# RWKV's y in a hybrid decoder step: products with the state over 128 rows, a decay vector per head, and other scheduling numbers

## The chip, the core and the metric

One core of one Trainium2 chip runs the whole program. The metric is the time of one execution in microseconds. The median of three runs before the change is 1459.84 us (1459.55 to 1460.57). Names of engines: PE is the matmul engine (PEld its weight loads), DVE the vector engine, ACT the activation engine, POOL the general-purpose engine, SP the engine that issues all DMAs here.

## What is computed

One layer of a decoder with two branches on the same input: gated linear attention (GLA) and RWKV-7. Their outputs are gated, projected up, merged, projected out and normalised. The prompt has 1024 tokens of 1024 columns; 8 sample tokens ride along. The branch that the change touches is the recurrence of RWKV-7, with 16 heads of 64:

```python
def _rwkv7_scan(r, w, k, v, kk, a, S0):
    def step(S, inp):
        rt, wt, kt, vt, kkt, at = inp
        sa = jnp.einsum('bhvk,bhk->bhv', S, -kkt)
        S = S * wt[:, :, None, :] + sa[..., None] * (kkt * at)[:, :, None, :] + vt[..., None] * kt[:, :, None, :]
        y = jnp.einsum('bhvk,bhk->bhv', S, rt)
        return S, y
    ...
p = jnp.einsum('btd,dn->btn', x, w_in)
...
y, S_rwkv = _rwkv7_scan(rh, hr(w), kh, vh, kk, hr(a), S_rwkv0.astype(jnp.float32))
```

`p` is the projection of x by w_in (9360 columns); by far the most matmuls of the kernel are this projection.

## The kernel before

**Passes and blocks.** The tokens are taken in two passes of 512 (PASS; the first has the 8 sample tokens as well). In each pass w_in is worked off in blocks of 128 columns (`blocks`). A block is 24 matmuls per stretch of tokens: each fp32 operand is split into two fp32r parts (xh and xl, and w's two parts in wpart), and three products are made for each of 8 row tiles. The first pass takes stretches of 256 and 264 tokens, the second one of 512. After both passes come the up-projections and the output projection.

**The pairs.** The 16 heads are handled as 8 pairs per pass, so 16 pairs in all. A pair's 128 partitions are two heads of 64 (HS). Time is cut into chunks of C = 64 tokens, NCH = 8 of them per pass. A pair runs through four parts:
- `front` (L1167 on): decays and keys on DVE and ACT; AZ, BK and `pc`, the decay over a whole chunk, [128, 8] (L1215); the products BK by AZ on PE (big<-az,wide in the profile); then the inversion of a triangular matrix per chunk. For that the 32x32 blocks go through HBM (LD by SP's DMAs into a tile of tag wide), POOL runs 62 instructions (tiles X and Xt), and the result goes back through HBM (XD) into XT and Yd.
- `back`: DVE transposes blocks of XT into Xd, PE multiplies (big<-Xd,Ld, then big<-Yd,Xt), and DVE multiplies AZ by `pc` into GG (tag gg).
- `turn`: transposes.
- `chain` (L1342 on): the recurrence over the 8 chunks. Each step has three matmuls of 128x130 in the one bank pch, with an evacuation between them: pch<-wide,gg gives `rh` (ACT or DVE copies it), pch<-rh,XT gives `u` (two copies of 64x65, one per head), and pch<-wide gives the state's change. Beside them ACT computes the decayed state s0 = u * pc (gg<-wide,pc in the profile), which DVE adds to the third product. After the 8 steps y is made by 32 matmuls in one bank: for each chunk and head one with the state (L1377, big<-az,gg) and one with u (L1379, big<-gg,wide).

The product with the state takes, for head h, only the 64 rows of that head: `d.s0[hs, x, ...]` by `AZ[hs, x, 1]`, a form of the PE array of 64 rows by 64 columns. The product with u takes all 128 rows by 64 columns, since GG holds zeros where it must.

**What sets the order.** The five engines run instruction streams that are fixed when the program is built. `Order.run` builds them: generators (streams) offer one operation each, and the one with the lowest key is issued next. The key is the modelled start time, less a priority (PRIO, FOR_PE), with additions for changes of the PE array's form (SWITCH), table loads of ACT (TABLE, AGE) and other things (ASIDE, URGENT, BIAS). `E` operations may go to DVE or POOL, `C` operations to ACT or DVE: the one that would end earlier by the model takes them. Nearly every instruction is issued by one helper and has the line L227 in the profile, so groups are told apart by their tiles.

Of the kernel before, what the change touches and what calls it, by code (L numbers as in the profile page):

```python
# [14 lines left out]
AF = mybir.ActivationFunctionType  # L15
# [5 lines left out]
P = 128  # L21
# [5 lines left out]
HT = TP // 2  # L27
# [5 lines left out]
C = 64  # L33
CV = C + 1
NCH = HT // C
# [10 lines left out]
HALF = HT + NS  # L46
SBUF = {
    "row": ([P, HALF], 40), "wide": ([P, NCH * 2 * CV], 4), "gg": ([P, NCH * 4 * CV], 2), "lw": ([P, HT], 2),
    "l2s": ([P, 2 * P], 1), "pc": ([P, NCH], 3), "az": ([P, 2 * HT], 2), "X": ([P, 256], 1),
    "Xt": ([P, P], 1), "Ld": ([P, P], 2), "S": ([P, GDV], 2), "Sp": ([P, CV], 2), "rh": ([P, 2 * CV], 2), "vm": ([P, NCH], 2),  # L50
    "sto": ([P, P], 1), "bnd": ([P, 1], 3), "st": ([P, 32], 3), "part": ([P, HALF], 2), "l2p": ([P, 2 * P], 2),
    "pair": ([P, 2, HT // 32], 3),
# [13 lines left out]
IDLE = 3  # L66
RANKW, RANKM = 48, 66
SPARE_ROWS = 11
EARLY_GATES = 13


HOP = {"P": 0.2, "D": 0.418, "G": 0.115, "V": 0.064, "A": 0.14}
# [2 lines left out]
HOLD = 0.11  # L75
TABLE = 1.28

AGE = 1.045

SPARE = 0.411  # L80
LANDED = 0.648
BIAS = 0.193
ASIDE = 8.388

PRIO = {"evacuate": 0.39, "pair": 0.3, "turn": 0.5, "chain": 0.42, "norm": 0.1, "x": 0.61, "lora": 0.42, "rank":
        1.25, "head": 0.27, "gate": -0.38, "w": 0.3, "out": 0.04, "state": -0.13, "block": -0.38}
FOR_PE = {"pair": 1.0, "turn": 1.84, "chain": 0.8, "norm": 0.39, "lora": 0.29, "rank": 1.85, "head": 0.89, "gate":
        1.0, "state": 2.11, "out": 0.05}
STAND, SCARCE, PER_ROW = 0.034, 0.249, 0.148

URGENT = 1.707
SIGMOID, EXP = "sigmoid_and_others", "natural_log_exp_and_others"
SETS = {AF.Sigmoid: SIGMOID, AF.Tanh: SIGMOID, AF.Exp: EXP, AF.Ln: EXP}

HS = (slice(0, 64), slice(64, 128))
# [144 lines left out]
def together(ops):  # L240

    op = ops[0]
    fns = [x.fn for x in ops]
    op.ways = [(op.eng, lambda: [fn() for fn in fns], sum(x.cost for x in ops))]
    op.ins = [y for x in ops for y in x.ins]
    op.outs = [x.out for x in ops]
    op.eng, op.fn, op.cost = op.ways[0]
    return op


class Stream:
# [4 lines left out]
    def be(self, name):  # L256
        self.kind, self.prio, self.for_pe = name, PRIO[name], FOR_PE.get(name, 0.0)


class Order:  # L260
# [83 lines left out]
    def start(self, op):  # L344

        best = None
        for eng, fn, cost in op.ways:
# [17 lines left out]
            if len(op.ways) > 1:  # L365
                end += BIAS if eng == "V" and "A" in op.ways[0][0] else ASIDE if eng == "G" and "G" in op.port else 0.0
            if best is None or end < best[0]:
# [13 lines left out]
    def run(self):  # L381
        while self.streams:
# [3 lines left out]
            for s in before:  # L386
                self.advance(s)
                if s.op is not None:
# [5 lines left out]
                    if s.kind in self.urgent:  # L394
                        key -= URGENT
                    if s.op.table not in (None, self.table):
                        key += max(0.0, TABLE - AGE * s.op.late)
                    if best is None or key < best[0]:
# [32 lines left out]
class Kern(Order):  # L431
# [735 lines left out]
    def front(self, c, p, st, d):  # L1167
        a, A, V, E = self.a, self.A, self.V, self.E
        BK_, L_ = yield from self.get("wide", 2)
        az, gg = (yield from self.get("az")), (yield from self.get("gg"))  # L1170
        BK = BK_[:, :2 * HT].rearrange("p (c t) -> p c t", c=NCH)
        AZ, g4 = az.rearrange("p (c s t) -> p c s t", c=NCH, s=2), gg.rearrange("p (c k z) -> p c k z", c=NCH, k=2)
# [12 lines left out]
        def bc(ap):  # L1185
            return ap.rearrange("p (c t) -> p c t", t=C)
        ta, tb, td, te, Pc_ = yield from self.rows(5)
        ts, tb, Pc_ = (x[:, :NCH * (C + 1)] for x in (ta, tb, Pc_))
        ta, td, te = (x[:, :HT] for x in (ta, td, te))
        ts3, tb3, Pc = (x.rearrange("p (c t) -> p c t", t=C + 1) for x in (ts, tb, Pc_))  # L1190
# [21 lines left out]
        yield V.scalar_tensor_tensor(td, td, -1.0, ta, ALU.mult, ALU.mult)  # L1212
        yield E.tensor_mul(kb, kb, te)
        yield E.tensor_mul(AZ[:, :, 1], bc(r), Pc[:, :, 1:])
        pc = yield from self.get("pc")  # L1215
        yield E.tensor_copy(pc, tb3[:, :, 0])

        for h, hs in enumerate(HS):
            yield E.tensor_mul(BK[hs, :, h * C:h * C + C], bc(td)[hs], tb3[hs, :, 1:])
# [16 lines left out]
        for n, y in enumerate(p4):  # L1236
            x, h = H * (n // 2), n % 2
# [9 lines left out]
        Ld_ = yield from self.get("Ld")  # L1247
# [7 lines left out]
        X = X_.rearrange("p (i t) -> p i t", t=32)  # L1255
# [13 lines left out]
        XT = (yield from self.get("XT")).rearrange("p (c h t) -> p c h t", c=NCH, h=2)  # L1269
# [5 lines left out]
        Yd_ = yield from self.get("Yd")  # L1275
        Yd = Yd_.rearrange("p (g x t) -> p g x t", g=4, t=32)
        H = NCH // 2
        for q in range(2):
# [3 lines left out]
                yield self.S.dma_start(XT[HS[h]][b, :, h, b], XD[n * NCH:(n + 1) * NCH].rearrange("c s t -> s c t"))  # L1282
            for x in range(0 if q else H):
                yield self.S.dma_start(Yd[32 * x:32 * x + 32, :, x], XD[2 * NCH + x:4 * NCH:H].rearrange("g s t -> s g t"))
        d.AZ, d.BK, d.G, d.XT, d.v, d.bonus, d.pc, d.L, d.Ld, d.Yd = AZ, BK, GG, XT, st[2], st[1], pc, L_, Ld_, Yd_
        d.y = Pc_[:, :HT]

    def back(self, d):
        GG, XT = d.G, d.XT

        H = NCH // 2
        Xd_ = yield from self.get("Xd")
        Xd = Xd_.rearrange("p (x g t) -> p x g t", g=4, t=32)
        q = [slice(32 * n, 32 * n + 32) for n in range(4)]
        for h in range(2):
            for n in range(2):
                g = 2 * h + n
                yield self.V.transpose(Xd[q[g], :, g], XT[q[2 * h], H * n:H * n + H, h, 0:32])
        pA = yield from self.bank("big", [P, P])
        yield together([self.P.matmul(pA[q[x]], d.Ld[:, x * 32:x * 32 + 32], Xd_[:, x * P:x * P + P], start=True, stop=True)  # L1300
                        for x in range(H)])
        As = yield from self.get("Xt")
        yield self.C.copy(As, pA)
        self.free(pA, Xd_, d.Ld)
        pZ = yield from self.bank("big", [P, P])
        yield together([self.P.matmul(pZ[q[g]], As[:, g * 32:g * 32 + 32], d.Yd[:, g * P:g * P + P], start=True, stop=True)
                        for g in range(4)])
        pZ3 = pZ.rearrange("p (x t) -> p x t", t=32)
        for h in range(2):
            for n in range(2):  # L1310
                yield self.C.copy(XT[q[2 * h], H * n:H * n + H, h, 32:64], pZ3[q[2 * h + n]])

        for h, hs in enumerate(HS):
            yield self.E.tensor_mul(GG[hs, :, 0, h], d.AZ[hs, :, 0], d.pc[hs].unsqueeze(2).to_broadcast([C, NCH, C]))
        self.free(pZ, As, d.Yd)

    def turn(self, d):
# [24 lines left out]
    def chain(self, c, p, d):  # L1342
        A, V = self.A, self.V
        AZ, BK, GG, XT, pc = d.AZ, d.BK, d.G, d.XT, d.pc
        u_, bt_ = d.u, BK

        for h, hs in enumerate(HS):
            if c.i:
                yield self.S.dma_start(u_[hs, 0, h], self.Sp[p][hs])
            else:  # L1350
                yield self.E.memset(u_[hs, 0, h], 0.0)
        S = yield from self.get("Sp")
        uf = u_.rearrange("p c h v -> p c (h v)")

        for x in range(NCH):
            u, s0 = u_[:, x], d.s0[:, x].rearrange("p (h v) -> p h v", h=2)
            pr = yield from self.bank("pch", [P, 2, CV])
            yield self.P.matmul(pr, GG[:, x, 0], u, start=True, stop=True)
            rh = yield from self.get("rh")
            yield self.C.copy(rh, pr.rearrange("p h v -> p (h v)"))  # L1360
            self.free(pr)
            yield A.activation(s0, u, AF.Copy, scale=pc[:, x:x + 1])
            pu = yield from self.bank("pch", [P, 2, CV])
            yield self.P.matmul(pu, XT[:, x], rh, start=True, stop=True)
            self.free(rh)
            for h, hs in enumerate(HS):
                yield self.C.copy(u[hs, h], pu[hs, h])
            self.free(pu)
            pS = yield from self.bank("pch", [P, 2, CV])
            yield self.P.matmul(pS, bt_[:, x], u, start=True, stop=True)  # L1370
            for h, hs in enumerate(HS):
                un = u_[hs, x + 1, h] if x + 1 < NCH else S[hs]
                yield V.tensor_add(un, pS[hs, h], s0[hs, h])
            self.free(pS)
        pY = yield from self.bank("big", [P, NCH, C])
        vs = [slice(1 + h * C, 1 + h * C + C) for h in range(2)]
        yield together([self.P.matmul(pY[hs, x], d.s0[hs, x, vs[h]], AZ[hs, x, 1], start=(x == 0), stop=False, skip_group_check=True)  # L1377
                        for x in range(NCH) for h, hs in enumerate(HS)] +
                       [self.P.matmul(pY[hs, x], uf[:, x, vs[h]], GG[:, x, 1, h], start=False, stop=True, skip_group_check=True)  # L1379
                        for x in range(NCH) for h, hs in enumerate(HS)])  # L1380
        yield self.C.copy(d.y, pY.rearrange("p c t -> p (c t)"))
        self.free(pY)
        self.free(AZ, BK, u_, GG, XT, pc)
        if c.i:
            self.spawn(self.state(p, S), "state")
        else:
            yield self.S.dma_start(self.Sp[p], S)
            self.free(S)
# [153 lines left out]
    def load_gates(self):  # L1542

        yield lambda: self.ctx[1].fronts >= NPAIR - 1
        for n in range(2):
            for c in self.ctx:
                for x in range(NK):
                    if x == EARLY_GATES:
                        yield lambda: self.ctx[1].fronts == NPAIR and self.ctx[1].gated == NPAIR + 2 * GH
# [308 lines left out]
```

## Time and profile before

| what | value |
|---|---|
| median of the runs | 1459.84 us |
| the profiled execution's own time | 1459.23 us |
| its span, first to last instruction | 1457.3 us |
| PE busy | 1443.5 us, 99% |
| DVE busy | 1058.8 us, 73% |
| ACT busy | 828.9 us, 57% |
| POOL busy | 362.6 us, 25% |
| granted clock of PE | 0.998 |

How to read the lines below: in a table of busy time by stretch, a row has the stretch, its length, then busy time and instruction count in the order of the engines. In a list of waits: who waited for whom, us in total, times, longest. In a timeline: start, duration, engine, line, operation, output<-input, for PE the rows*columns of the array in use, and the count of merged records. In a list of groups: engine, operation, tiles, shapes, count, then busy us and the mean ns of one. One fp32 matmul is two records on PE, one fp32r matmul is one.

### The profile page before, as it was taken

The numbers are of one execution on the slowest core, as the hardware profiler recorded it, in microseconds if no ns is written. First come the engines' busy times: TensorE is split into PE (matmuls) and PEld (weight loads), VectorE is DVE, ScalarE is ACT, GpSimd is POOL, SyncE is SP. The second block draws the span as 40 slices with busy tenths as digits, with TensorE's granted clock in tenths as the row PEclk, the third lists the DMA queues.
The fourth block names the chain that finished last, engine by engine and source line by source line (L and its number), as shares of the span: only waits on it lengthen the run. The fifth ranks groups of instructions, "written<-read, shape, count | busy, mean of one in ns | idle before, by whom it ended". The sixth has DMA issues, their size and how long they took to land.

```text
span 1457.3 us, 30477 instructions
## 1 busy us (share of the span) xinstructions
PE 1443.5 (99%) x10768; PEld 1280.5 (88%) x10768; DVE 1058.8 (73%) x2208; ACT 828.9 (57%) x2114; POOL 362.6 (25%) x1111
## 2 busy tenths in 40 slices
PE   9999999999999999999999999999999999999997
PEld 8999999999999998878888888888788898898786
DVE  6687487958895889577747895787669856665665
ACT  5656667766776677455555565464557646643210
POOL 1060506050604160406051405411332330000000
PEclk9999999999999999999999999999999999999999
DMA  8786887678767885675466455746575768798432
GB/s 308 262 289 201 287 275 269 202 245 297 253 209 241 277 307 191 190 210 186 137 205 208 152 173 175 229 138 207 185 230 156 226 206 249 250 311 287 135 119 84
DMA packets 211315, 319.14 MB, mean 219 GB/s; under 512 B 91699, under 2 KB 107196, under 8 KB 211164
## 3 DMA queue, kind: packets, MB, share of 16 engines
q1 hardware_dynamic: 211164, 317.20, 67.6%
q8 instruction: 86, 1.41, 0.4%
q14 instruction: 65, 0.53, 0.1%
HBM read 197.45 MB, written 118.61 MB: 217 GB/s over the span
## 4 chain that ended last, share of the span: by engine, by line
PE 92%; DVE 3%; DMA 3%; ACT 1%; issue 1%; SPq 1%; DVEq 0%; ACTq 0%
PE proj L227 59%; PE big L227 27%; PE pch L227 6%; DVE row L227 1%; SPq L227 1%; DVE xl L227 0%; DMA wraw<-w_in 0%; DMA wide<-LD 0%; DVE wpart L227 0%; DMA row<-xT 0%; DMA wraw<-w_up_gla 0%; DMA row<-o_gla 0%; DMA wide<-Sp 0%; DVE XT L227 0%; DMA w<-wpart 0%
## 5 line engine op out<-in xcount | busy, mean ns | idle before, releaser
L227 PE MATMUL proj<-xh,wpart 128*128 128x264 f32 (+2 forms) x3696 | 901.3, 328 | 0.0
L227 PEld LDWEIGHTS proj<-xh,wpart 128*128 128x128 f32 x3696 | 614.2, 188 | 49.0 <-issue 6.5
L227 PE MATMUL proj<-xl,wpart 128*128 128x264 f32 (+2 forms) x1848 | 603.8, 327 | 0.0
L227 PEld LDWEIGHTS proj<-xl,wpart 128*128 128x128 f32 x1848 | 348.1, 188 | 23.6 <-issue 1.4
L227 POOL TENSOR_TENSOR Xt<-X,wide 128x60 f32<-128x60 f32 (+24 forms) x496 | 170.9, 344 | 676.5 <-DMA wide<-LD 281.4
L227 DVE TENSOR_TENSOR row<-row 128x256 f32<-128x256 f32 (+10 forms) x369 | 191.1, 530 | 14.6 <-ACT row L227 8.0
L227 DVE TENSOR_TENSOR wpart<-wraw,wpart 128x512 fp32r<-128x512 f32 x210 | 146.1, 698 | 74.4 <-ACT wpart L227 71.2
L227 ACT CAST wpart<-wraw 128x512 fp32r<-128x512 f32 x210 | 130.0, 621 | 100.1 <-PE proj L227 57.6
L227 POOL TENSOR_TENSOR X<-X,Xt 128x60 f32<-128x60 f32 (+24 forms) x496 | 170.3, 343 | 38.7
L227 ACT ACTIVATE row<-row 128x520 f32<-128x520 f32 (+4 forms) x229 | 137.7, 612 | 13.3 <-DMA row<-sg 5.6
L227 PE MATMUL big<-xh,wpart 128*128 128x256 f32 (+2 forms) x576 | 133.0, 320 | 0.2 <-DVE wpart L227 0.2
L227 PEld LDWEIGHTS big<-xh,wpart 128*128 128x128 f32 x576 | 95.3, 188 | 7.4 <-DVE wpart L227 0.4
L227 DVE TENSOR_TENSOR wide<-pch,gg 64x65 f32<-64x65 f32 x224 | 49.8, 222 | 65.1 <-PE pch L227 62.9
L227 ACT COPY row<-big 128x128 f32<-128x128 f32 (+6 forms) x152 | 49.7, 356 | 81.1 <-PE big L227 77.0
L227 PE MATMUL big<-xl,wpart 128*128 128x256 f32 (+2 forms) x288 | 92.2, 320 | 0.8 <-DVE xl L227 0.8
L227 DVE SCALAR_TENSOR_TENSOR row<-proj,pv,row 128x255 f32<-128x255 f32 (+1 forms) x95 | 54.6, 575 | 48.2 <-ACT tail L227 36.4
L227 ACT COPY rh<-pch 128x130 f32<-128x130 f32 x121 | 32.5, 268 | 98.8 <-PE pch L227 98.0
L227 ACT COPY wide<-pch 64x65 f32<-64x65 f32 x241 | 50.1, 208 | 50.4 <-PE pch L227 47.4
L227 ACT ACTIVATE row<-proj,omu 128x256 f32<-128x256 f32 (+1 forms) x95 | 52.2, 549 | 33.5 <-PE proj L227 32.5
L409 ACT ACT_TABLE_LOAD x54 | 69.3, 1283 | 0.9
L227 PE MATMUL big<-row 128*64 128x64 f32 (+4 forms) x648 | 65.0, 272 | 0.2 <-DVE gg L227 0.2
L227 PEld LDWEIGHTS big<-xl,wpart 128*128 128x128 f32 x288 | 54.2, 188 | 5.3 <-DVE xl L227 1.8
(234 smaller groups left out, 2069.6 us busy)
## 6 DMA issues: line engine op xcount, KB each, us to landing
w<-wpart SPq DMA_DIRECT2D x146, 512.0 KB, 4.3
wpart<-w SPq DMA_DIRECT2D x146, 512.0 KB, 3.8
wraw<-w_in SPq DMA_DIRECT2D x146, 256.0 KB, 4.2
wide<-LD SPq DMA_DIRECT2D x64, 128.0 KB, 3.8
wraw<-w_up_gla SPq DMA_DIRECT2D x32, 256.0 KB, 3.7
wraw<-w_up_rwkv SPq DMA_DIRECT2D x32, 256.0 KB, 3.7
sg<-row SPq DMA_DIRECT2D x16, 260.0 KB, 3.2
row<-sg SPq DMA_DIRECT2D x16, 260.0 KB, 4.3
```

Of the source, the lines that this page charges most:

```text
L227: ways.append((eng, lambda call=call: call(out, *args, **kw), price(eng, name, out, args, ins)))
L409: self.nc.scalar.preload_act_table_set(self.table)
```

## The change

`pc` becomes [128, 8, 2], one column per chunk and head. A memset makes it zero, and two copies put each head's decay into that head's own rows. In `chain` the scaling by `pc` becomes two activations of 128x65, one per head: each zeroes the rows of the other head. So the product with the state can take all 128 rows, in the same form of the PE array as the product with u. In `back` the multiplication of GG takes its head's column. The numbers of the scheduler are set anew as well.

```diff
-    "l2s": ([P, 2 * P], 1), "pc": ([P, NCH], 3), "az": ([P, 2 * HT], 2), "X": ([P, 256], 1),
+    "l2s": ([P, 2 * P], 1), "pc": ([P, NCH * 2], 3), "az": ([P, 2 * HT], 2), "X": ([P, 256], 1),
...
-EARLY_GATES = 13
+EARLY_GATES = 14
...
-ASIDE = 8.388
+ASIDE = 10.306
...
-        pc = yield from self.get("pc")
-        yield E.tensor_copy(pc, tb3[:, :, 0])
+        pc_ = yield from self.get("pc")
+        pc = pc_.rearrange("p (c h) -> p c h", h=2)
+        yield E.memset(pc_, 0.0)
+        for h, hs in enumerate(HS):
+            yield E.tensor_copy(pc[hs, :, h], tb3[hs, :, 0])
...
-            yield self.E.tensor_mul(GG[hs, :, 0, h], d.AZ[hs, :, 0], d.pc[hs].unsqueeze(2).to_broadcast([C, NCH, C]))
+            yield self.E.tensor_mul(GG[hs, :, 0, h], d.AZ[hs, :, 0], d.pc[hs, :, h:h + 1].to_broadcast([C, NCH, C]))
...
-            yield A.activation(s0, u, AF.Copy, scale=pc[:, x:x + 1])
+            for h in range(2):
+                yield A.activation(s0[:, h], u[:, h], AF.Copy, scale=pc[:, x, h:h + 1])
...
-        yield together([self.P.matmul(pY[hs, x], d.s0[hs, x, vs[h]], AZ[hs, x, 1], start=(x == 0), stop=False, skip_group_check=True)
+        yield together([self.P.matmul(pY[hs, x], d.s0[:, x, vs[h]], AZ[:, x, 1], start=(x == 0), stop=False, skip_group_check=True)
```

The other numbers that move are AGE, BIAS, URGENT, PER_ROW and the entries pair, gate and out of FOR_PE. Three places show what becomes of the order.

ACT in a step of the chain of the second pair, before: `rh` is the evacuation of the first product, `gg<-wide,pc` the decayed state, `wide<-pch` the two copies of u; what stands between them are evacuations of other work (`row<-proj` and `row<-big`, projections and GLA).

```order
L227 COPY rh<-pch 128x130
L227 ACTIVATE gg<-wide,pc 128x130
L227 ACTIVATE row<-big,pv 128x128
L227 ACTIVATE row<-proj,omu 128x264
L227 COPY wide<-pch 64x65 x2
```

The same step of ACT now:

```order
L227 COPY rh<-pch 128x130
L227 ACTIVATE gg<-wide,pc 128x65 x2
L227 ACTIVATE row<-big,b_glaeps 128x264
L227 COPY wide<-pch 64x65 x2
L227 ACTIVATE row<-row 128x520
```

The decayed state is two instructions at the same place, and other evacuations stand beside it.

POOL between two pairs, before: the last instructions of one pair's inversion, and the first of the next (X is set to zero and to the identity).

```order
L227 TENSOR_TENSOR Xt<-X,wide 128x8
L227 TENSOR_TENSOR X<-X,Xt 128x8
L227 MEMSET wide 64x65
L227 MEMSET X 128x256
L227 MEMSET X 32x8 x4
```

POOL at the same place now:

```order
L227 TENSOR_TENSOR Xt<-X,wide 128x8
L227 TENSOR_TENSOR X<-X,Xt 128x8
L227 MEMSET pc 128x16
L227 MEMSET X 128x256
L227 MEMSET X 32x8 x4
```

The memset of `pc` for the next pair stands directly behind the inversion of the last one. All 16 memsets of `pc` went to POOL; the 32 copies are on DVE.

PE at the tenth pair's first matmul on the inverse (big<-Xd,Ld), before, among projection matmuls of the second pass:

```order
L227 MATMUL proj<-xh_9043,wpart 128x512
L227 MATMUL big<-part,headsr 128x512
L227 MATMUL proj<-xl_9060,wpart 128x512
L227 MATMUL proj<-xh_9043,wpart 128x512
L227 MATMUL big<-Xd_185,Ld 32x128 x4
L227 MATMUL proj<-xh_9051,wpart 128x512
L227 MATMUL big<-part,headsr 128x512
```

PE at the same place now:

```order
L227 MATMUL proj<-xh_8977,wpart 128x512
L227 MATMUL proj<-xh_8985,wpart 128x512
L227 MATMUL proj<-xl_8998,wpart 128x512
L227 MATMUL proj<-xh_8985,wpart 128x512
L227 MATMUL big<-Xd_185,Ld 32x128 x4
L227 MATMUL proj<-xh_8991,wpart 128x512
L227 MATMUL proj<-xl_9007,wpart 128x512
```

It stands at another row tile of the block (xh_8985 is the third of eight, xh_9043 was the sixth), and between the pair's products for the inversion and this place there are now 174 matmuls of 512 columns instead of 192. PE has 9093 matmuls before and after.

More of the change, by code (lines that the diff above doesn't have):

```diff
@@ L76 @@
 TABLE = 1.28
-AGE = 1.045
+AGE = 1.059
 SPARE = 0.411
 LANDED = 0.648
-BIAS = 0.193
-ASIDE = 8.388
+BIAS = 0.21
+ASIDE = 10.306
 PRIO = {"evacuate": 0.39, "pair": 0.3, "turn": 0.5, "chain": 0.42, "norm": 0.1, "x": 0.61, "lora": 0.42, "rank":
         1.25, "head": 0.27, "gate": -0.38, "w": 0.3, "out": 0.04, "state": -0.13, "block": -0.38}
[L87 to L91, printed above, removed]
+FOR_PE = {"pair": 1.08, "turn": 1.84, "chain": 0.8, "norm": 0.39, "lora": 0.29, "rank": 1.85, "head": 0.89, "gate":
+        1.07, "state": 2.11, "out": 0.26}
+STAND, SCARCE, PER_ROW = 0.034, 0.249, 0.167
+URGENT = 2.231
 SIGMOID, EXP = "sigmoid_and_others", "natural_log_exp_and_others"
@@ L1284, in front @@
                 yield self.S.dma_start(Yd[32 * x:32 * x + 32, :, x], XD[2 * NCH + x:4 * NCH:H].rearrange("g s t -> s g t"))
-        d.AZ, d.BK, d.G, d.XT, d.v, d.bonus, d.pc, d.L, d.Ld, d.Yd = AZ, BK, GG, XT, st[2], st[1], pc, L_, Ld_, Yd_
-        d.y = Pc_[:, :HT]
+        d.AZ, d.BK, d.G, d.XT, d.v, d.bonus, d.pc_, d.L, d.Ld, d.Yd = AZ, BK, GG, XT, st[2], st[1], pc_, L_, Ld_, Yd_
+        d.y, d.pc = Pc_[:, :HT], pc
     def back(self, d):
@@ L1382, in chain @@
         self.free(pY)
-        self.free(AZ, BK, u_, GG, XT, pc)
+        self.free(AZ, BK, u_, GG, XT, d.pc_)
         if c.i:
```

## The prediction

> **What bounds the kernel now.** I read the page first, then busy time by stage, then the waits of the engines, and at the end single places in the timeline.
>
> ```profile
> span 1457.3 us, 30477 instructions
> PE 1443.5 (99%) x10768; PEld 1280.5 (88%) x10768; DVE 1058.8 (73%) x2208; ACT 828.9 (57%) x2114; POOL 362.6 (25%) x1111
> ```
>
> PE is busy for 99% of the span; no other engine comes near. The table of busy time by stage says where PE's 13.8 idle us are:
>
> ```profile
> 50.00:700.00 650.00, 648.51 (x5671) 606.68 (x5670) 494.65 (x1068) 419.31 (x1148) 207.62 (x625) 1.00 0.74 241
> 700.00:1260.00 560.00, 558.52 (x3725) 467.78 (x3724) 405.15 (x853) 314.77 (x771) 150.76 (x471) 1.00 0.63 195
> ```
>
> The second number is PE's busy time. From 50 to 1260 us, where all the chains lie, PE is idle for 1.49 + 1.48 = 3.0 us; the rest of its idle time is at the two ends, and there the change does nothing. So a change moves the time only if it changes how long PE's own stream takes, or if it makes PE wait. A matmul counts as busy until its modelled end, past the start of the next one, so short waits hide in the busy time; the weight loads (PEld) show them better:
>
> ```profile
> PEld big L227 <- DVE gg L227: 2.2, 5, 0.6
> PEld big L227 <- DVE xl L227: 1.8, 4, 0.6
> ...
> PEld big L227 <- DVE part L227: 1.4, 3, 0.9
> ```
>
> These are the three longest in total that another engine ended after the start; the first column is us in all, then how often, then the longest. They come to 5.4 us. That is about what a better order could still win.
>
> **The products of y on PE.** Today the 16 products with the state (64 rows by 64 columns) stand ahead of 16 products of 128 rows by 64 columns. This is the first pair's place:
>
> ```profile
> 168.84 1.15 PE L227 MATMUL big<-az,gg 64*64 64x64 f32 x32
> 169.92 1.15 PE L227 MATMUL big<-gg,wide 128*64 128x64 f32 x32
> 171.00 0.39 PE L227 MATMUL proj<-xh,wpart 128*128 128x256 f32 x1
> ```
>
> Each matmul is two records. From start to start both groups take 1.08 us, whatever their rows. Their pace without a change of form is read by counting records in windows of two lengths, two of them inside each group:
>
> ```profile
> 169.00:169.35 0.35, 0.35 (x16) 1.00 1.07 416
> 169.00:169.70 0.70, 0.70 (x28) 1.00 1.08 427
> 170.05:170.40 0.35, 0.35 (x16) 1.00 1.01 413
> 170.05:170.75 0.70, 0.70 (x28) 1.00 0.98 380
> ```
>
> 0.35 us more hold 12 records more, 29.2 ns each, in the form with 64 rows and in the one with 128. A group of 32 needs 0.93 us, and the 0.15 us left of 1.08 go to the change from one form of the array to the next. With the change all 64 records have one form: 64 x 29.2 ns plus one change of form, 2.01 us, instead of 2.16. That is 0.147 us less per pair, and 16 x 0.147 = 2.35 us in all, on PE's own path. The new order spends some of it: counted over PE's whole stream, the form of the array changes 216 times before and 204 times now, so 16 changes go and 4 come elsewhere. 12 x 0.147 = **1.8 us less**. That the wider form has twice the rows costs nothing by these rows.
>
> One rule of the skill speaks against this. The Trainium skill, "TensorE: Matmul & The Clock Gate", Part 3 (packing small matmuls), states that a weight load overlaps matmuls in flight only when its row group differs. The two heads' products lay on different rows of the array and would now share all of them. By that rule 32 loads of 0.134 us would stand bare, 4.3 us instead of 0.9, and over the 16 pairs the sum would be some 52 us slower instead of 1.8 us faster. The trace does not agree: in the group that has the new form already, 32 loads take 1.01 us.
>
> ```profile
> 169.91 1.01 PEld L227 LDWEIGHTS big<-gg,wide 128*64 128x64 f32 x32
> L227 PEld LDWEIGHTS big<-az,gg x512: 129/134/135, 168.8 to 1258.5; 64*64 64x64 f32 x171
> ```
>
> **The scaled state on ACT.** One activation of 130 columns per step becomes two of 65, 128 more in all.
>
> ```profile
> L227 ACT ACTIVATE gg<-wide,pc 128x130 f32<-128x130 f32 x128 | 52.2, 408 | 0.9 <-PE pch L227 0.8
> L227 ACT COPY wide<-pch 64x65 f32<-64x65 f32 x241 | 50.1, 208 | 50.4 <-PE pch L227 47.4 <-DVE wide L227 0.2
> L227 ACT COPY rh<-pch 128x130 f32<-128x130 f32 x121 | 32.5, 268 | 98.8 <-PE pch L227 98.0
> ```
>
> Halving 130 columns took 268 - 208 = 60 ns off a copy, so a half should take 408 - 60 = 348 ns. One step as it ran:
>
> ```profile
> 601.21 0.41 ACT L227 ACTIVATE gg<-wide,pc 128x130 f32<-128x130 f32 x1
> ...
> 602.49 0.43 ACT L227 COPY wide<-pch 64x65 f32<-64x65 f32 x2 [0.87 <-PE pch L227]
> ...
> 603.80 0.46 DVE L227 TENSOR_TENSOR wide<-pch,gg 64x65 f32<-64x65 f32 x2 [3.56 <-PE pch L227]
> ...
> 605.36 0.41 ACT L227 ACTIVATE gg<-wide,pc 128x130 f32<-128x130 f32 x1
> 605.66 0.15 ACT L227 COPY tail<-proj 128x1 f32<-128x1 f32 x1
> ```
>
> ACT's next instruction starts 0.30 us after the activation, so a half holds ACT for 0.24 us. Per step this is 0.48 - 0.30 = 0.18 us more, and 2 x 0.348 - 0.408 = 0.29 at most if nothing overlaps: 23 to 37 us of ACT in 128 steps. I take 23, since the overlap is measured. I count 10 table loads fewer in the new order, which give back some of it:
>
> ```profile
> L409 ACT ACT_TABLE_LOAD x54 | 69.3, 1283 | 0.9
> ```
>
> That is 12.8 us, so ACT's 57% rise by a point. On the path I take **nothing**. The scaled state was done at 601.62 and read at 603.80, and DVE had waited for PE, not for it; the second half ends 0.18 us later. The copies behind it began after 0.87 us of idling for PE. Such waits of ACT on the chain's products sum to 98.0 and 47.4 us (the rows of the copies above). Without this cover it would cost up to 128 x 0.18 = 23 us. It cannot gain.
>
> **The decay vector.** Each pair gets a memset and two copies for one.
>
> ```profile
> L227 DVE COPY pc<-row x16: 159/165/324, 51.8 to 1122.1; 128x8 f32<-128x8 f32 x16
> L227 POOL MEMSET row<- 128x8 f32 x10 | 1.2, 118 | 0.0
> 899.73 0.21 POOL L227 TENSOR_TENSOR X<-X,Xt 128x8 f32<-128x8 f32 x1
> 905.88 0.32 DVE L227 COPY pc<-row 128x8 f32<-128x8 f32 x1
> ```
>
> DVE gets 16 x 0.165 = 2.6 us, 5.2 if the added copy took the longest time, on an engine with 27% to spare. The memset (16 x 0.12 = 1.9 us) goes to POOL, in the order shown above directly behind the last pair's inversion. DVE's copies now wait for POOL, and behind them in DVE's queue stand the products for the next pair and the weight splits that PE needs. POOL's inversion ended at 899.94 and the copy came at 905.88: 5.9 us of cover, the least of the 15 places. If POOL came later than that, each us would hold DVE for one. I take nothing.
>
> **The order anew.** The instructions are otherwise the same; the scheduler's numbers move nearly all of them by a little. No row of before prices that. It is bounded on the side of a gain by the 5.4 us above, on the side of a loss by the two places where the new order is tightest (rival 2). I take zero.
>
> The sum is -1.8 us. The profiled execution took 1459.23 us, 1.9 more than its span, and would take 1457.5. It is 0.6 us under the median 1459.84, so for the median I predict **1458.1 us**.
>
> **Rivals.** What a measurement of this kernel can tell from no change is 0.2%, 2.9 us.
>
> *1. The new order also takes waits out of PE's stream.* For it: 5.4 us of them are there, and 1.1 us beyond my sum is enough for faster by over 0.2%. Against: PE already idles only 3.0 us in 1210. Half of them would make 2.7 + 1.8 = 4.5 us less: 1455.3.
>
> *2. PE comes to the inverse too early.* Between a pair's products for the inversion (big<-az,wide) and the first matmul on its result (big<-Xd,Ld), the way is LD by DMA, POOL, and back by DMA. Three passages of before, by their first and last rows; the third is the shortest of the 16:
>
> ```profile
> 582.85 0.72 PE L227 MATMUL big<-az,wide 64*128 64x128 f32 x8
> 641.19 0.42 PE L227 MATMUL big<-Xd,Ld 128*32 128x128 f32 x8
> 715.46 0.38 PE L227 MATMUL big<-az,wide 64*128 64x128 f32 x2
> 774.49 0.32 PE L227 MATMUL big<-Xd,Ld 128*32 128x128 f32 x4
> 992.94 0.49 PE L227 MATMUL big<-az,wide 64*128 64x128 f32 x4
> 1050.09 0.43 PE L227 MATMUL big<-Xd,Ld 128*32 128x128 f32 x8
> 1380.00:1400.00 20.00, 20.00 (x89) 16.23 (x88) 9.16 (x15) 0.99 (x4) 0.00 (x0) 1.00 0.27 91
> ```
>
> They took 58.3 us (eighth pair), 59.0 (tenth) and 57.2. In the new order the tenth pair has 174 projection matmuls of 512 columns there instead of 192. At 20 us for 88 of them, 0.23 us each, PE arrives 4.1 us sooner, after 54.9. The eighth has 153 instead of 180, 6.2 us less, and 19 other matmuls more: at the 0.06 us of two records of y's products at least 1.1 us, and I take 2.2, so 4 us sooner, after 54.3. If the inversion needs what its shortest took, PE stands 2.3 + 2.9 = 5.2 us with everything behind it. Net +3.4: 1463.2. It decides for slower once the two cost 4.7 us. Against: the transfers may now come sooner as well.
>
> *3. ACT's longer queue delays evacuations or the chain.* If a fifth of the 23 us reached PE: +4.6 - 1.8 = +2.8, 1462.6; a quarter would be over 0.2%. The waits of ACT for PE speak against it.
>
> *4. With shared rows the weight loads stand bare after all:* 32 loads of 0.134 us for 0.93 us per pair, 16 x 3.4 = 54 us slower, 1510. The row of 32 loads in 1.01 us speaks against it. This is what the rule above would give.
>
> **The numbers.** Forecast 0.42; rival 1 0.35; rival 2 0.15; rival 3 0.07; rival 4 0.01. Faster by over 0.2% is rival 1: 0.35. Within 0.2% is the forecast: 0.42. Slower holds the other three: 0.23. The range leaves out the far ends of rivals 1 and 3 and all of 4: low 1453.0 (1458.1 - 5.1, nearly all of the 5.4), high 1464.5 (rival 2 with a us more for a third place). The forecast's own range is 1456.9 to 1462.7.
>
> **What would show it.** In the profile after: y's products with the state as 128*64, with 64 records in one group of about 2.0 us; gg<-wide,pc 256 times near 350 ns; ACT near 840 us; PE's idle time between 50 and 1260 us still near 3 us. I am wrong if the group of 64 takes 2.16 us or more, if PE's weight loads wait for ACT rh or ACT gg (rival 3), if they wait for DVE Xd or for As at the eighth and tenth pair (rival 2), or if the three waits shrink by more than 1 us (rival 1).

## The result: slower by a quarter of a per cent, and the profile after

The changed kernel took 1463.07 us in the median of 9 runs, the kernel before 1459.55 us beside it. The ratio is 1.0026, interval [1.0017, 1.0034]: 3.8 us slower, on the side to which the prediction gave 0.23, inside its range. One of the nine runs took 2355.93 us at a granted clock of 0.556 and is not in the ratio. The profiled execution took 1462.86 us. Its page has two rows that answer to the first fence of the prediction:

```profile
span 1461.1 us, 30673 instructions
PE 1444.7 (99%) x10768; PEld 1277.0 (87%) x10768; DVE 1065.7 (73%) x2227; ACT 836.7 (57%) x2223; POOL 354.0 (24%) x1133
```

The products of y did what was predicted. The first pair's place in the timeline of PE, and the weight loads of the same place:

```profile
177.98 1.15 PE L227 MATMUL big<-az,gg 128*64 128x64 f32 x32
178.96 1.10 PE L227 MATMUL big<-gg,wide 128*64 128x64 f32 x32
179.99 0.40 PE L227 MATMUL proj<-xh,wpart 128*128 128x264 f32 x1
...
177.97 1.01 PEld L227 LDWEIGHTS big<-az,gg 128*64 128x64 f32 x32
```

From 177.98 to 179.99 the 64 records took 2.01 us, the number predicted (2.16 before). The 32 loads of the new products, whose rows are now shared by both heads, take 1.01 us like those of the products with u. The rule on row groups (the Trainium skill, "TensorE: Matmul & The Clock Gate", Part 3) would have made them 4.3 us; this trace does not agree with it.

ACT is as predicted too: 256 activations near 350 ns, and the engine at 836.7 us:

```profile
L227 ACT ACTIVATE gg<-wide,pc 128x65 f32<-128x65 f32 x256 | 75.8, 347 | 0.2
L409 ACT ACT_TABLE_LOAD x44 | 56.5, 1283 | 0.7
```

A part of what went wrong is seen in the busy time by stretch, PE's first:

```profile
50.00:700.00 650.00, 648.72 (x5647) 605.41 (x5646) 490.21 (x1050) 424.69 (x1199) 206.16 (x634) 1.00 0.74 242
700.00:1260.00 560.00, 556.43 (x3685) 464.04 (x3684) 413.93 (x883) 314.37 (x820) 143.58 (x483) 1.00 0.61 190
```

The last three numbers of such a row are PE's granted clock, the busy share of the DMA engines and the GB/s that they moved. PE's idle time from 50 to 700 us is 1.28 us (1.49 before). From 700 to 1260 us, in the second pass, it is 3.57 us (1.48 before). That is 1.9 us more in all. PE's busy time grew as well, from 1443.5 to 1444.7 us, though the products of y now take about 2 us less; so some of the loss lies in short waits inside the busy time, and these rows do not place it. The waits of PE name what is new in the second pass; before, the first of these rows had 0.4 us and the second did not exist:

```profile
PE pch L227 <- DMA wide<-Sp: 1.3, 1, 1.3
PE proj L227 <- DMA wpart<-w: 0.7, 1, 0.7
```

Both are DMAs: the state that a pair takes over from the first pass (Sp, into the chain's tile of tag wide), and weights. The state's place, first in SP's queue and then on PE:

```profile
1065.70 2.54 SPq L227 DMA_DIRECT2D Ld<-gg  x4
1069.45 1.75 SPq L227 DMA_DIRECT2D wide<-LD  x4
1071.72 1.13 SPq L227 DMA_DIRECT2D wide<-Sp  x2
...
1076.43 0.40 PE L227 MATMUL proj<-xh,wpart 128*128 128x512 f32 x1
1078.14 0.46 PE L227 MATMUL pch<-wide,gg 128*128 128x130 f32 x2 [1.31 <-DMA wide<-Sp]
```

The chain's first product would have begun at about 1076.8, when the matmul of 1076.43 ended; it began at 1078.14. The state's two DMAs were issued only at 1071.72, behind the next pair's transfers for the inversion (Ld, and wide from LD). Before, SP had the same pair's state ahead of those:

```profile
1059.67 1.14 SPq L227 DMA_DIRECT2D wide<-Sp  x2
1060.90 0.53 SPq L227 DMA_DIRECT2D LD<-gg  x1
...
1064.43 0.39 PE L227 MATMUL pch<-wide,gg 128*128 128x130 f32 x2
```

There 4.8 us from issue to use were enough without a wait in the row. In the new order 5.1 us were not, with other transfers ahead of it. The DMA engines too were fuller: their share was 1.02 from 1071.7 to 1078.2 us, and 0.71 before from 1059.6 to 1064.4. Which of the two made the load late was not separated. A load that comes late cannot be seen in an order of instructions on PE; it has to be looked for in what SP and the DMA engines have in front of it.

### The profile page after: what moved, and what is told of

Its sections match the earlier page's. It is cut to its first block, busy times and chain, and to the rows that moved or that the text cites. A ratio compares the mean times of both kernels' runs of the same rounds, so it can differ in the third digit from the quotient of the medians.

```text
span 1461.1 us, 30673 instructions
## 1 busy us (share of the span) xinstructions
PE 1444.7 (99%) x10768; PEld 1277.0 (87%) x10768; DVE 1065.7 (73%) x2227; ACT 836.7 (57%) x2223; POOL 354.0 (24%) x1133
## 4 chain that ended last, share of the span: by engine, by line
PE 85%; DVE 3%; DMA 2%; SPq 1%; ACT 1%; issue 0%; DVEq 0%
PE proj L227 54%; PE big L227 25%; PE pch L227 6%; DVE row L227 1%; SPq L227 1%; DVE wpart L227 0%; DMA wide<-Sp 0%; DMA row<-o_gla 0%; DMA row<-o_rwkv 0%; DMA XD<-X 0%; DMA wpart<-w 0%; DVE XT L227 0%; DVE part L227 0%; DVE wide L227 0%; ACT row L227 0%
## 5 line engine op out<-in xcount | busy, mean ns | idle before, releaser
L227 PE MATMUL proj<-xh,wpart 128*128 128x256 f32 (+2 forms) x3712 | 904.8, 328 | 1.0 <-DMA wpart<-w 0.7
L227 POOL TENSOR_TENSOR Xt<-X,wide 128x60 f32<-128x60 f32 (+24 forms) x496 | 163.5, 330 | 699.4 <-DMA wide<-LD 123.4
L227 DVE TENSOR_TENSOR row<-row 128x512 f32<-128x512 f32 (+10 forms) x369 | 190.0, 528 | 18.7 <-ACT row L227 7.8
L227 ACT ACTIVATE row<-row 128x520 f32<-128x520 f32 (+3 forms) x229 | 137.7, 611 | 15.1 <-DMA row<-sg 7.6
L227 PE MATMUL big<-xh,wpart 128*128 128x264 f32 (+2 forms) x560 | 129.0, 318 | 0.7 <-ACT xh L227 0.4
L227 ACT COPY row<-big 128x128 f32<-128x128 f32 (+7 forms) x147 | 48.9, 357 | 76.8 <-PE big L227 74.1
L227 ACT ACTIVATE gg<-wide,pc 128x65 f32<-128x65 f32 x256 | 75.8, 347 | 0.2
L227 PE MATMUL big<-row 128*64 128x64 f32 (+5 forms) x652 | 66.3, 273 | 0.5 <-DVE gg L227 0.5
```

The source lines that it names most:

```text
L227: ways.append((eng, lambda call=call: call(out, *args, **kw), price(eng, name, out, args, ins)))
```

## The experiments

All ratios are to the kernel before, with 95% intervals. "Before's order" below means that every instruction stands where it stood before; an operation that becomes two is issued at the place of the one.

**All three parts in before's order.** The operations' emitting functions are replaced after they are planned, so that the scheduler sees the old ones:

```diff
+            plan = A.activation(s0, u, AF.Copy, scale=pc[:, x, 0:1])
+            def halves(s0=s0, u=u, x=x):
+                for h in range(2):
+                    self.nc.scalar.activation(s0[:, h], u[:, h], AF.Copy, scale=pc[:, x, h:h + 1])
+            plan.ways = [(eng, halves, cost) for eng, _, cost in plan.ways]
```

> All three parts of the change (products of 128 rows, the decay vector per head, two activations), with every instruction at the place that the order of before gives it. Theory A (the parts are worth what the sum said, the loss comes from the new order): 16 changes of form fewer at 0.147 us, 2.35 us less than before, 1457.2, ratio 0.998. Rival B (the extra work on ACT or the wait for POOL's memset reaches PE): 1462 or more, ratio 1.002 or more, and waits of PE on the chain's evacuations in the profile.

Measured: 1460.22 us, 1.0005 [0.9996, 1.0013]. It lies between the two ends. So 3.1 of the 3.8 us lost (1.0026 - 1.0005, some 1.8 us to a side) come with the new order, but the gain of the wide products is gone in the old order too. One new wait of PE stands in the first pair's chain, where ACT has the copy to `rh` behind a cast of weights:

```profile
162.99 0.49 PE L227 MATMUL pch<-rh,XT 128*128 128x130 f32 x2 [0.81 <-ACT rh L227]
```

Two other new waits are 0.9 us for the state's load (at 931.83 us) and 0.4 us for weights. The same two stretches as above, in this run:

```profile
50.00:700.00 650.00, 646.16 (x5661) 604.54 (x5660) 495.64 (x1073) 428.27 (x1208) 206.87 (x634) 1.00 0.74 241
700.00:1260.00 560.00, 557.98 (x3689) 466.69 (x3689) 406.20 (x860) 327.07 (x837) 150.74 (x477) 1.00 0.64 194
```

PE idles here for 3.84 + 2.02 = 5.9 us, more than the 4.9 us of the changed kernel, and yet this run is shorter, since PE's busy time is 1442.6 us against 1444.7. So idle time alone does not show what the new order costs.

**The numbers alone, and the code alone.** The first has before's code with the new scheduling numbers, the second the new code with before's numbers:

```diff
-EARLY_GATES = 13
+EARLY_GATES = 14
...
-ASIDE = 8.388
+ASIDE = 10.306
```

> The code of before with the new scheduling numbers alone; the form of the array changes 212 times. Theory A: the order that these numbers make has new waits, so 4 to 6 us slower than before less 0.6 us for 4 changes of form, 1463 to 1465, ratio 1.0025 to 1.0035. Rival C (the numbers fit, and it is the new code's shift of all places that hurt): as before, 1459, ratio 0.999 to 1.001.

> The new code with the old scheduling numbers; the order is made anew, and the form changes 194 times. Theory A (the numbers are at fault): 22 changes of form fewer, 3.2 us less, 1456.3, ratio 0.998. Rival C (any shift of the order brings waits at new places): 1460 to 1464, ratio 1.0005 to 1.003.

Measured: the numbers alone 1471.12 us, 1.008 [1.0066, 1.0095]; the code alone 1505.22 us, 1.0309 [1.0296, 1.0322]. Both are far worse than the two together, and outside all that was expected. The waits of PE in the second begin:

```profile
PE big L227 <- ACT part L227: 6.2, 1, 6.2
PE pch L227 <- ACT wide L227: 4.0, 6, 0.9
...
PE pch L227 <- DMA wide<-Sp: 3.2, 1, 3.2
```

Here neither set of numbers gave a good order for the code of the other. "The order anew" is not a small term that can be put at zero beside the others: these orders lie up to 45 us above before's. Not all of that is waiting: in the profile of the code alone the clock granted to PE stood at 0.5 for 44 us within the span, and in that of the numbers alone for 10 us. If PE's work goes with the clock, half of these 44 and 10 us are lost, at most 22 and 5 us (an estimate). Before and in the changed kernel it never stood at 0.5 between 10 and 1450 us.

**The products narrow again in the new order.**

```diff
-        yield together([self.P.matmul(pY[hs, x], d.s0[:, x, vs[h]], AZ[:, x, 1], start=(x == 0), stop=False, skip_group_check=True)
+        yield together([self.P.matmul(pY[hs, x], d.s0[hs, x, vs[h]], AZ[hs, x, 1], start=(x == 0), stop=False, skip_group_check=True)
```

> The changed kernel with every instruction at its place, only the 16 products with the state take 64 rows again. Theory A: the change of form comes back 16 times, 2.35 us more than the changed kernel: 1465.4, ratio to before 1.004. If the saving were hidden behind a wait in this order: as the changed kernel, 1463. The profile shows besides which waits of PE come back at the same places in a second execution of this order (the state's load at 1078 us, the weights' at 918 us): if they are the order's, both do.

Measured: 1466.1 us, 1.004 [1.0027, 1.0053], so 0.14% or 2.0 us above the changed kernel, near the 2.35 us of 16 changes of form; with some 2.3 us to a side this alone would not tell it from nothing. The two waits on DMAs come back at the same places of this order: 1.12 us at the state's place (1080.28 us, where the profile names DVE as the last to release) and 0.44 us at the weights' (919.79 us).

**The wide products alone in before's order.** One activation of 130 columns and the old decay column stay, so y holds a part of the other head: the output differs, the instructions and their sizes are those meant.

```diff
-        yield together([self.P.matmul(pY[hs, x], d.s0[hs, x, vs[h]], AZ[hs, x, 1], start=(x == 0), stop=False, skip_group_check=True)
+        ops = [self.P.matmul(pY[hs, x], d.s0[:, x, vs[h]], AZ[:, x, 1], start=(x == 0), stop=False, skip_group_check=True)
```

> The kernel before with its order, only the 16 products with the state take 128 rows; without zeros in the other head's rows, y holds a part of the other head as well. Theory A: 16 changes of form at 0.147 us go, 2.35 us less, 1456.9, ratio 0.9984. If the form were worth nothing: 1459.3, ratio 1.000.

Measured: 1456.67 us, 0.9979 [0.997, 0.9988], 3.0 us less. The term of the products is real and reaches the end of the program.

**The two activations alone in before's order.** The edit is that of the first experiment with the old column as scale.

> The kernel before with its order, only the decayed state is computed by two activations of 65 columns, both with the same decay. The kernel with all three parts in the old order took 1 us more than before, not 2.35 less. Theory F (ACT's longer queue reaches PE): 2.5 to 3.5 us more, 1462 to 1463, ratio 1.002, with a wait of PE on ACT rh near 163 us. Rival G (the cost lies in the decay vector, its memset on POOL and DVE's wait): 1459.3, ratio 1.000.

Measured: 1460.53 us, 1.0004 [0.9996, 1.0013], 0.6 us more. The wait on ACT rh near 163 us is only 0.2 us here, and it is 0.5 us with the wide products alone, where ACT does what it did before. So the halves do not make it.

**Both of these together.**

> The wide products and the two half activations in the order of before, without the decay vector (so y holds a part of the other head, and the output differs). Theory D (the decay vector is what eats the gain): the two add up, -3.0 + 0.6 = -2.4 us, 1457.2, ratio 0.998. Theory N (the parts do not add up): within 1 us of the run with all three parts, 1459.5 to 1461, ratio 1.000 or above.

Measured: 1458.6 us, 0.9986 [0.9978, 0.9995], 2.0 us less. They add up within their intervals. What takes the gain away comes with the decay vector.

**The decay vector alone.** A memset on POOL and two copies on DVE in place of one:

```diff
+            self.nc.gpsimd.memset(pc_, 0.0)
+            for h, hs in enumerate(HS):
+                self.nc.vector.tensor_copy(pc[hs, :, 0], tb3[hs, :, 0])
```

> Only the decay vector per head, in the order of before: the memset on POOL, two copies for one on DVE and the strided read of it; the activation (130 columns) and the products (64 rows) stay those of before, and both copies write the same column. In the old order the wide products alone gave -3.0 us, the halves alone +0.6, all three parts +0.8. Theory D (the +3 us that are missing belong to the decay vector: DVE stands for POOL at the first copy, and what is queued behind it comes late): +2.5 to +3.5 us, 1462 to 1463.5, ratio 1.002. Theory N (it costs nothing, as I had put it, and the loss is of the three together, in places where PE had just been in time): within 0.6 us of before, ratio 1.000.

Measured: 1461.35 us, 1.0009 [1.0, 1.0018], 1.3 us more: less than theory D said, and by its interval not safely more than N. PE's idle time in the first pass went from 1.49 to 2.86 us:

```profile
50.00:700.00 650.00, 647.14 (x5661) 605.33 (x5661) 495.79 (x1075) 417.49 (x1145) 207.20 (x634) 1.00 0.74 241
```

One place, the sixth pair's, shows how. First DVE before, around the copy, with the busy time of all engines in the 29 us around it (DVE's is the third of the five, 28.25 us):

```profile
405.00:434.00 29.00, 29.00 (x260) 27.35 (x260) 28.25 (x57) 21.67 (x57) 0.74 (x5) 1.00 0.58 188
421.64 0.17 DVE L227 COPY pc<-row 128x8 f32<-128x8 f32 x1
421.72 1.38 DVE L227 TENSOR_TENSOR gg<-az,pc 64x512 f32<-64x512 f32 x2
423.12 1.99 DVE L227 TENSOR_TENSOR wide<-row 64x512 f32<-64x512 f32 x3
```

The same place of DVE with the decay vector, and PE ten us later:

```profile
422.41 0.34 DVE L1222 COPY pc<-row 64x8 f32<-64x8 f32 x2
422.76 1.39 DVE L227 TENSOR_TENSOR gg<-az,pc 64x512 f32<-64x512 f32 x2
424.16 1.99 DVE L227 TENSOR_TENSOR wide<-row 64x512 f32<-64x512 f32 x3
...
433.15 0.51 PE L227 MATMUL big<-part,headsr 128*128 128x512 f32 x1 [0.28 <-DVE part L227]
```

From the first copy to the product on gg there were 0.08 us, now 0.35: 0.27 us more. That is more than the 0.17 us of one copy, because the single copy over 128 partitions let the next instruction start 0.09 us before it ended, and copies over 64 do not (see the last section). Over all 16 pairs the time from the first copy to the next instruction is 5.8 us instead of 1.5. DVE has no gap to absorb them in this stretch, and PE waits 0.28 us for `part`, which stands behind in DVE's queue. At none of the 16 places does a copy wait for the memset: DVE works up to the copies without a gap.

**The copies three times.** The two copies of the run above are issued three times over; the rest is that run.

```diff
+            for _ in range(3):
+                for h, hs in enumerate(HS):
+                    self.nc.vector.tensor_copy(pc[hs, :, 0], tb3[hs, :, 0])
```

> The decay vector alone in the order of before, and each of its two copies on DVE issued three times (the last leaves what the first left): four copies more per pair than with the vector alone, about 0.6 to 0.7 us of DVE per pair where it has no gaps (two copies took 0.34 us in its row of 2). Theory D (the copies cost by delaying what is queued behind them on DVE in stretches where it never idles; with the vector alone this was 0.27 us at the first pair's place, and five places where PE stands grew by 0.1 to 0.4 us each, 1.2 us in all): 2 to 4 us slower than the vector alone, 1463.3 to 1465.3, ratio 1.0025 to 1.004 against before. Theory N (the +1.3 of the vector alone is the scatter of the interval): within 0.7 us of it, ratio 1.0005 to 1.0014.

Measured: 1470.74 us, 1.0078 [1.0065, 1.0091], 10 us above the vector alone, three times what theory D said. The same place of DVE and of PE:

```profile
425.45 1.13 DVE L1223 COPY pc<-row 64x8 f32<-64x8 f32 x6
...
436.97 0.51 PE L227 MATMUL big<-part,headsr 128*128 128x512 f32 x1 [1.06 <-DVE part L227]
```

0.79 us more of copies (1.13 - 0.34) made 0.78 us more of waiting (1.06 - 0.28). Over 16 pairs the copies are 16 x 0.79 = 12.6 us more, and 10 us of them reach the end (some 2.3 us to a side). So the copies' time on DVE costs, and it needs neither the memset nor the strided read of the column, of which this run has no more. The share that reaches the end isn't fixed: of the first 4.3 us it was 1.3.

**The copies taken off DVE.** In before's order with all three parts, DVE does the one full copy of before and its product reads that. The vector per head is copied from it by ACT, in front of the chain's first activation, or by POOL, beside the instructions that fill the chain's first state:

```diff
+            self.nc.vector.tensor_copy(pcf, tb3[:, :, 0])
...
+                        self.nc.scalar.copy(pc[hs, :, h], d.pcf[hs])
```

```diff
+            def spread(fn, h=h, hs=hs):
+                fn()
+                self.nc.gpsimd.tensor_copy(pc[hs, :, h], d.pcf[hs])
```

> All three parts in the order of before, but DVE does the one full copy of before and its product reads that; the two copies that make the vector per head are on ACT, in front of the chain's first activation (about 0.2 us each, 16 x 0.4 = 6 us of ACT in all). Theory D: the copies' 1.2 us on DVE go, and what the wide products and the halves gave together (-2.0 us) is left: 1457.0 to 1458.0, ratio 0.9985 to 0.999. Theory N: as with all three parts, 1460.2, ratio 1.0005; or slower still if the first step of the chain has no cover for 0.4 us on ACT (8 x 0.4 = 3.2 us at most, 1463).

> The same, with the two copies on POOL, beside the instructions that fill the chain's first state (in the first pass these stand directly ahead of the next pair's inversion). Theory D: as on ACT, 1457.0 to 1458.0, ratio 0.9985 to 0.999. Rival: POOL stands for DVE's copy with the inversion queued behind it, and PE gets the inverse late: some us slower, 1462 or more, with PE waiting for the inverse (big on Xd and Ld).

Measured: on ACT 1462.03 us, 1.0016 [1.0008, 1.0025]; on POOL 1458.07 us, 0.9991 [0.9983, 1.0]. On ACT the 32 copies of 0.197 us cost no less than on DVE (1.0005 there); theory D's forecast for ACT failed. In its profile PE waits 1.0 us in the chain for DVE's sums (0.2 in the first run); whether that carries the cost was not taken apart. On POOL the copies cost little, and the rival with the inverse did not come. The place of DVE and PE again, on POOL:

```profile
421.40 0.17 DVE L1222 COPY pc<-row 128x8 f32<-128x8 f32 x1
421.48 1.38 DVE L227 TENSOR_TENSOR gg<-az,pc 64x512 f32<-64x512 f32 x2
...
431.85 0.51 PE L227 MATMUL big<-part,headsr 128*128 128x512 f32 x1
L1363 POOL COPY pc<-pc x32: 184/190/1057, 103.3 to 1179.3; 64x8 f32<-64x8 f32 x32
```

The 0.08 us are back and PE's wait at this place is gone. This version computes all that the changed kernel does, is 5 us under the changed kernel by the medians and 1.3 us under before by the ratio, whose interval reaches 1.0.

**The state's loads earlier, in the new order.** The loads of Sp are issued when the pair leaves `back`, not at the chain's start:

```diff
+        if c.i:
+            u = d.L.rearrange("p (c h v) -> p c h v", c=NCH, h=2)
+            for h, hs in enumerate(HS):
+                self.nc.sync.dma_start(u[hs, 0, h], self.Sp[p][hs])
```

> The changed kernel with its order, only the second pass's loads of a pair's first state (wide<-Sp) are issued when the pair leaves back, some 10 us before its chain. Theory A (the new order lets transfers come after PE needs them): the wait of 1.3 to 1.7 us at 1078 us goes, so 1461.4 to 1461.8, ratio to before 1.0015. Rival D (PE's later waits only take its place): 1463, ratio 1.0026.

Measured: 1461.32 us, 1.0007 [0.9998, 1.0016]. By the ratios 0.19% or 2.8 us of the loss are gone, with some 1.8 us to a side; the wait that went is 1.3 us, and the profiled span is 1.0 us shorter, so more than the 1.3 us is not shown. The load moved from 1071.72 to 1063.32, and the chain's first product waits no more:

```profile
1063.32 1.13 SPq L1152 DMA_DIRECT2D wide<-Sp  x2
...
1076.26 0.38 PE L227 MATMUL pch<-wide,gg 128*128 128x130 f32 x2
```

**The same in before's order,** with all three parts, and with none.

> All three parts in the order of before, and the second pass's loads of the state issued when the pair leaves the step before its turn, instead of at the start of the chain. In the order of before with all three parts (1460.22, +0.8 us) the longest wait was PE for the state's transfer, 0.9 us, and the sum of DMA waits 1.3. Theory T (late transfers hold PE in that run too): 0.9 to 1.3 us less than it, 1459.0 to 1459.4, ratio 0.9995. Rival: the wait moves to the next thing that is late (as the weights issued first did), within 0.4 us of 1460.2.

> The kernel before, with only the second pass's loads of the state issued early, as in the run with all three parts. Before waits 0.4 us for that transfer once. Theory T: 0 to 0.4 us less, 1459.1 to 1459.5, ratio 0.9998; so a gain in the run with all three parts is that run's own late transfer and no general gain. Rival: the earlier issue on SP delays something else there, 0.5 us or more slower.

Measured: 1461.37 us, 1.0011 [1.0002, 1.002], against 1.0005 without it, so the gain that theory T expected isn't there; and 1459.59 us, 1.0002 [0.9993, 1.001]. With all three parts the wait of 0.9 us for the state is gone from the profile, and PE waits 1.4 us for another transfer (row<-OS, at 1218.44 us) instead: the rival's reading. In before's order an earlier issue brought nothing; only in the new order did it help. But a late load of the state was not the new order's alone, since the first run had one too.

**The weights ahead of the inverse's transfers, in the new order.** At one place SP issues a weight load before two DMAs of XT and one of Yd.

```diff
+                op.ways = [(eng, lambda fn=fn: (fn(), self.release()), cost) for eng, fn, cost in op.ways]
```

> The changed kernel with its order, only at the one place near 912 us SP issues the reload of weights (wpart<-w) ahead of three DMAs of the inverse (two XT, one Yd), which wait for XD. Theory A (the reload is late because it stands behind a waiting DMA in SP's queue): the two waits of PE on it at 914 and 918 us, 1.3 us together, go: 1461.8, ratio 1.0017. Rival E (the reload is late because its buffer is freed late or the DMA engines are full): the waits stay, 1463, and the inverse may come later as well.

Measured: 1462.66 us, 1.0023 [1.0014, 1.0032], no gain. The place before the edit, and then with it:

```profile
916.64 0.43 PE L227 MATMUL big<-Xd,Ld 128*32 128x128 f32 x8
918.24 0.50 PE L227 MATMUL proj<-xh,wpart 128*128 128x512 f32 x1 [0.75 <-DMA wpart<-w]
```

```profile
917.77 0.43 PE L227 MATMUL big<-Xd,Ld 128*32 128x128 f32 x8 [1.06 <-DVE Xd L227]
```

The wait moved from the weights to the inverse. SP's queue did not hold the inverse back: the first DMA of XT was issued at 912.83 us in the one and at 912.84 in the other. But DVE's first transpose of XT came 1.70 us after that issue in the one and 3.63 us in the other, and the DMA engines' share from 912 to 915 us was 0.36 in the one and 0.80 in the other. That the weights in flight slowed the inverse's transfers fits these numbers, as rival E had it; it was not tried by itself. PE is there too early for both.

## Where the prediction was right, and which step failed

**The products of y: right.** The group took 2.01 us as worked out. 2.35 us were put on 16 changes of form; 3.0 us [1.8 to 4.4] were gained by them in before's order, and some 2.0 in the new one. Rival 4 is out (its 54 us would have made 1512, not 1510).

**The halves on ACT: right.** Nothing was put on the path; 0.6 us [-0.6, 1.9] were measured, so rival 3 with its 4.6 us is out. Its sign shows only faintly: in the changed kernel PE's weight loads wait once for ACT gg, 0.4 us.

**The decay vector: wrong, though the size is small.** The step that failed is "on an engine with 27% to spare", from which nothing was taken. The share is a mean over 1457 us; in the 29 us around the copy of one pair DVE is busy for 28.25. The cover named (5.9 us of POOL ahead of the copy) was for the memset, and the memset never mattered. The queue that stands behind the copies on DVE was named and not priced. The copies cost 1.3 us alone [0 to 2.6], and 2.8 us where the wide products and the halves are in already (1.0005 against 0.9986). The prediction's own 16 x 0.165 = 2.6 us of DVE was the bound to carry into the range; measured, the copies hold DVE for 16 x 0.27 = 4.3 us more.

**The order anew: wrong, and the larger miss.** "I take zero" was worth +3.1 us (some 1.8 to a side). The bound on the side of loss was looked for at the inverse. These are the passages of the eighth and the tenth pair from the products to the first matmul on the inverse in the changed kernel:

```profile
591.25 2.06 PE L227 MATMUL big<-az,wide 64*128 64x128 f32 x32
645.51 0.43 PE L227 MATMUL big<-Xd,Ld 128*32 128x128 f32 x8
727.69 2.06 PE L227 MATMUL big<-az,wide 64*128 64x128 f32 x32
781.59 0.42 PE L227 MATMUL big<-Xd,Ld 128*32 128x128 f32 x8
```

They took 54.3 and 53.9 us; 54.3 and 54.9 had been forecast, and PE waited at neither. So the step "if the inversion needs what its shortest took" failed: 57.2 us was how long PE had left it, not how long it needed. A wait of PE of 1.1 us for the inverse showed in the run with the weights first, at the twelfth pair. Rival 2 had the right kind of cause (PE comes too early for transfers) at the wrong transfers: the state's load, issued earlier, gave back the 1.3 us of its wait, and 2.8 us by the ratios. Where the rest of the 3.1 us arises stays open: it is not in PE's idle time, which was longer still with all three parts in before's order. Rival 1 is out: PE's idle time grew.

**The sum.** In before's order -3.0, +0.6 and +1.3 make -1.1 us, and all three together measured +0.8. The difference of 1.9 us is open: each interval is about 1.3 us to a side, the wait of 0.9 us for the state is in that run and in none of the three others, and the one for `rh` is 0.8 us there and 0.2 to 0.5 in them. The order's +3.1 is the rest of the 3.8 us by definition, and no check of the sum. That the decay vector costs in the new order what it costs in the old wasn't tried.

## What to carry to other kernels

An engine's mean share says little about what one more instruction costs: take the busy time of the few tens of us around it, and if that is full, the time for which it holds the engine (from its start to the next one's) times its count is the bound. When an order changes, look in SP's queue at what stands ahead of each load that a chain starts with, and at how full the DMA engines are there, and not only at the place of its user. The time that one engine leaves another is no measure of what that other needs.

## What was not expected of the hardware

A copy on DVE takes 0.17 us with 64x8 elements and 0.165 us with 128x8, so that halving the partitions saves nothing, and six of them in a row hold DVE for 1.13 us. The split even costs more than a second copy. In the profile before, of instructions on DVE behind which the next one waits for nothing, those over 128 partitions let it start 0.08 us before their end (median of 317), and those over 64 only 0.014 us after it (median of 203). So a product of 128x512 holds DVE for 0.60 us and one of 64x512 for 0.69, though both take 0.68; and the copy of 128x8 holds it for 0.075 us and two copies of 64x8 for 0.35. The same copy takes 0.197 us on ACT and 0.190 us in the median on POOL, where the longest of 32 took 1.057 us. In the slowest order (the new code with the old numbers) the clock granted to PE was 0.95 in the mean after 1260 us, where it was 0.99 before:

```profile
1260.00:1500.00 240.00, 226.09 (x1213) 190.46 (x1211) 143.54 (x252) 85.20 (x193) 0.00 (x0) 0.95 0.57 188
1260.00:1457.00 197.00, 189.61 (x1026) 162.24 (x1025) 126.24 (x213) 63.00 (x127) 0.00 (x0) 0.99 0.58 193
```

Its longest stretch at 0.5, 17.1 us from 1169.7, began within PE's wait of 6.2 us, and others right behind waits of 1.5, 1.4 and 3.2 us (at 1209.4, 1258.0 and 1270.3). What makes it fall was not tried.
